# Rotary tables moved behind the last low part, x's norm spread over two engines, and idle matmuls ahead of the first products, in a two-layer decoder trunk

## The chip, the cores and the metric

The kernel runs on one core of one Trainium2 chip. Its time is the device time of one execution in microseconds (us), the median of several runs. TensorE is called PE in the profile's rows, VectorE DVE, ScalarE ACT, GpSimd POOL, SyncE SP; PEld is TensorE's loading of weights.

## The reference

Two layers of a decoder on a sequence of 512 tokens of width 2048, all in f32. The change lies in the opening of layer 0 and at the end of its first stage. Cut to what matters there:

```
c_act = silu(c)
mod = (c_act @ ada_w[i] + ada_b[i])                 # per layer: shift, scale, gate
h = rmsnorm(x, norm_g[i]) * (1.0 + scale) + shift
...
# layer 0: retention
proj = h @ w_in                                     # 2048 x (2048 q, 2048 k, 4096 v, 4096 g)
q = rope(q.reshape(B, S, RET_HEADS, RET_DK), pos)   # cos and sin of pos * inv_freq
k = rope(k.reshape(B, S, RET_HEADS, RET_DK), pos) * (RET_DK ** -0.5)
...
return (silu(g) * y) @ w_out
```

Layer 1 is a latent attention, and a last RMSNorm closes the trunk. x, the adaLN weights and a few constants also come in layouts prepared on the host (`x_t`, `ada_t`, `vecs`, `rot_c`).

## The kernel before

**Products in three parts.** Each f32 matrix is split into a high part (rounded to the fast matmul type, by a copy on ScalarE) and a low part (the rest, by a subtraction on VectorE); a product is then hi x hi, hi x lo and lo x hi. The profile shows the copies as CAST and the subtractions as TENSOR_TENSOR.

**The opening** (L439 to L556). Everything is transposed: `xT[u]` holds 2 x 128 channels of x against 512 tokens, u from 0 to 7. SP loads x, then the rows of the adaLN weights (`aw`, 1 MB each, four buffers) and the first weights (`v`, `g`, `qk`; three raw buffers). TensorE spreads c over all partitions (`c_ps`, L462), ScalarE puts it through silu into `c_all`, in four pieces. For x's norm ScalarE squares each `xT[u]` (`square`, L474), VectorE adds the squares up (`gather`), TensorE sums them over partitions into `x_sums` (`add_squares`), `rsqrt` takes the factor per token (a scaling on VectorE, a power on GpSimd), `spread_one` puts it on a diagonal (two blocks by ScalarE, two by VectorE) and TensorE spreads that over all partitions as `x_r`. `near` (tile x_near) is a copy of `x_r` in SBUF. `normalise` multiplies `xT` by it. A column of shift or scale is a weighted sum of an `aw` tile with `c_all` on VectorE (`sum_mod` whole, `sum_part` in halves), finished on ScalarE as b_col and a_col; `make_h` then makes h's high part (`hT`) and an f32 copy (`h_..f`) on ScalarE, from which VectorE makes the low part.

**The first stage** (L558 to L615) runs over eight units u of two channel blocks. Each unit multiplies h by three pieces of the input weights (the first head's q and k, its v, its g), 24 matmuls each. The 4 banks `acc` serve v and qk in turn: `swap` has ScalarE copy the partial sums out and the others back; g keeps the 4 banks `aux`. `prepare(u)` emits a unit's normalise, sums, casts and low parts, `load_unit` its loads. After unit 7, `hand_over` stores v (GpSimd's queue) and brings qk's partial sums back, and the last qk products run (`bank_products`).

**The rotary tables.** `rotary_tables` (L251) is a generator: a load of the positions, then steps of VectorE work (a multiply by the frequencies, a reduction of the angle in several parts, a clamp), at last two Sin activations on ScalarE. In the kernel before all of it is drawn in one go after `hand_over` (`for _ in tables`), the load on ScalarE's queue, and the two tables are stored to HBM by GpSimd's queue (`tables_d`).

**The order of the work.** `queued(fn)` ties each instruction that fn emits behind the last one emitted so far on its engine, for ScalarE, VectorE, TensorE and SP: each of these four queues runs in the order in which the code is written, and an instruction that waits holds up those behind it. After the first stage the memory pool `l0` is closed and `lp` opened in its place; a tile of `lp` must wait for the last user of the memory beneath it. Then a list of steps follows (the other heads' q and k, retention, layer 1); the main loop loads weights up to three units ahead and calls `prepare_for(i + 1)`, the casts and low parts of the next step, ahead of step i's matmuls. Ahead of the loop stand the first step's preparation and, by `keep_rows`, the evacuation of the first stage's banks: `qk0[b]` into tiles qk_st (0 and 2 in the pool base, 1 and 3 in `lp`), then g through silu (g_st). The first step's products take the `acc` banks as these come free.

Of the kernel before, what the change touches and what calls it, by code (L numbers as in the profile page):

```python
# [9 lines left out]
F32 = mybir.dt.float32  # L10
F32R = mybir.dt.float32r
I32 = mybir.dt.int32
# [4 lines left out]
P = 128  # L17
T = 512
# [31 lines left out]
def hybrid_trunk_kernel(  # L50
# [56 lines left out]
    def acc(name):  # L107
        return psum.tile([P, T], F32, tag="acc", bufs=4, name=name)
# [4 lines left out]
    def small(name, n=1):  # L113
        return base.tile([P, n], F32, tag="small", bufs=24, name=name)

    ident = base.tile([P, P], F32, name="ident")
# [3 lines left out]
    ones = base.tile([P, P], F32, name="ones")  # L120
    DVE.memset(ones, 1.0)
    mhalf = base.tile([P, NT], F32, name="mhalf")
# [127 lines left out]

    def rotary_tables(cos, sin, col, signed, name, queue):  # L251

        pos_i = base.tile([P, T], I32, tag="tmp", bufs=6, name=f"{name}_pi")
        queue.dma_start(pos_i, positions.rearrange("o t -> (o t)").partition_broadcast(P))
# [178 lines left out]
    def queued(fn, *args):  # L433
        with behind(A_, V_, T_, S_):
            return fn(*args)
# [24 lines left out]
    c_all = l0p.tile([P, D], F32, name="c_all")  # L460
    ACT.dma_start(c_all[0:1, :], c)
    c_ps = [acc(f"c_ps{j}") for j in range(4)]  # L462
    for j, ps in enumerate(c_ps):
# [10 lines left out]
    def square(u, j=slice(0, 2)):  # L474

        if u not in sq:
            sq[u] = k4b(f"x_sq_{u}", F32)
        ACT.activation(sq[u][:, j, :], xT[u][:, j, :], AF.Square)

# [12 lines left out]
    ret_tables = [rot(l0p, f"ret_{n}") for n in ("cos", "sin")]  # L492
    tables = rotary_tables(*ret_tables, 0, False, "ret", ACT)
    silus = {1: 0, 2: 1, 4: 2, 5: 3}
    for u in range(NU - 2):
# [6 lines left out]
    for j in range(2):  # L502
        queued(square, NU - 1, j)
    queued(gather, 0, 0, 1)
    queued(add_squares, 0, True, False)
    queued(gather, NU - 2, NU - 2, 1)
# [4 lines left out]
    def scaled_bias():  # L511
        DVE.scalar_tensor_tensor(
            out=bias1, in0=bias_c[0][:, KD:], scalar=1.0, in1=norm_c[0], op0=ALU.add, op1=ALU.mult
        )

    POOL.dma_start(c_d, c_all[0:1, :])
    queued(scaled_bias)
    queued(sum_part, 0, 0, 0)
    r_col = queued(rsqrt, x_sums[:, 0:NT], NT, 1.0 / D, "x")
    diag = tmp("x_diag")  # L520
    x_r, near = aux("x_r"), l0p.tile([P, T], F32, name="x_near")

    def spread_one(t):
        cols = slice(t * P, (t + 1) * P)
        if t % 2:
            DVE.tensor_scalar(out=diag[:, cols], in0=ident, scalar1=r_col[:, t : t + 1], scalar2=None, op0=ALU.mult)
        else:
            ACT.activation(diag[:, cols], ident, AF.Identity, scale=r_col[:, t : t + 1])
        PE.matmul(x_r[:, cols], ones, diag[:, cols], start=True, stop=True)

    def normalise(u, j=None):
# [4 lines left out]
        DVE.tensor_mul(v, v, r)  # L536

    for t in range(NT):
        queued(spread_one, t)
    low_v = queued(prepares["v", 0])  # L540
    queued(sum_part, 0, 0, 1)
    queued(sum_part, 0, 1, 0)
    queued(normalise, 0, 0)
    queued(ACT.copy, near, x_r)
    queued(sum_part, 0, 1, 1)
    low = queued(make_first, 0)
    queued(low_v)
    low_g = queued(prepares["g", 0])
    queued(low_g)
# [11 lines left out]
    def prepare(u):  # L561

        here, there = ("qk", "v") if u % 2 == 0 else ("v", "qk")
        queued(normalise, u)
# [15 lines left out]
    queued(products, "v", 0)  # L580
    queued(sum_mod, 1, 0)
    banks["g"] = [aux(f"g0_{b}") for b in range(4)]
    queued(products, "g", 0)
    queued(queued(prepares["qk", 0]))
    queued(normalise, 0, 1)
    queued(swap, "v", "qk")
    queued(sum_mod, 1, 1)
    low = queued(make_first, 1)
    queued(low)
    queued(products, "qk", 0)  # L590
    queued(products, "qk", 1)
# [4 lines left out]
    for u in range(1, NU):  # L596
# [9 lines left out]
        if more:  # L606
            queued(swap, here, there)
            prepare(u + 1)
        else:
            queued(hand_over)  # L610
            for _ in tables:
                pass
            for n, t in enumerate(ret_tables):
                POOL.dma_start(tables_d[n * P : (n + 1) * P, :], t)
        queued(bank_products, there, u)  # L615
    qk0, g0 = banks["qk"], banks["g"]
    l0.__exit__(None, None, None)


    lp = tc.tile_pool(name="lp", bufs=1)  # L620
    lpp = lp.__enter__()

# [1283 lines left out]
    n_loaded = 3  # L1906
    n_prepared = prepare_for(0)
    for b in range(4):
        queued(keep_rows, qk0[b], qk_d, b * P, f"qk0_st{b}", AF.Identity, in_turn(b))
# [276 lines left out]
```

## Time and profile before

| | |
|---|---|
| time, median of 3 runs | 2192.41 us (2191.99 to 2193.34) |
| the profiled execution: time, span | 2194.48 us, 2192.7 us |
| granted TensorE clock, mean | 0.995 |
| busy: TensorE, its weight loads, VectorE, ScalarE, GpSimd | 98%, 82%, 71%, 46%, 5% |
| HBM traffic | 200 GB/s over the span |

The span is the time from the first to the last instruction of the program; the time of an execution also holds what lies around it. A row of the timeline has the start in us, the duration in us, the engine (a q behind it: its queue issues a DMA), the line, the operation, the tiles written and read, the shapes, the number of instructions merged into the row, and in brackets how long the engine stood idle before and what it waited for. Instructions overlap by a little, so durations add up to somewhat more than the pitch of a series.

### The profile page before, as it was taken

Reading aid. Unit: us, or ns where it says so; the run is one execution under the profiler, and the core shown is the slowest. Engines: PE = TensorE matmul, PEld = TensorE weight load, DVE = VectorE, ACT = ScalarE, POOL = GpSimd, SP = SyncE. Lnnn points to the kernel's source line nnn. Section 1 sums busy time; section 2 is a strip of 40 time slices with the busy share of each in tenths; the row PEclk is TensorE's granted clock in tenths of the full one; section 3 lists DMA queues with packets and bytes.
Section 4 is the critical chain, followed back from the end, with each engine's and each line's share of the span. In section 5 each row is a group of like instructions: output and inputs, shape, how many; then the busy total and the mean of one; then the engine's idle time right before and its main releaser. Section 6 shows DMA issues by size and latency. Waiting matters only on the chain.

```text
span 2192.7 us, 27643 instructions
## 1 busy us (share of the span) xinstructions
PE 2149.2 (98%) x10176; PEld 1795.6 (82%) x10176; DVE 1563.2 (71%) x2312; ACT 1015.7 (46%) x1547; POOL 100.9 (5%) x175
## 2 busy tenths in 40 slices
PE   6998999999999999999999999999999999999997
PEld 4886888888888877888888888888888889888887
DVE  7976878677676788756677767657877677776545
ACT  6763344434343444433444535344444366664443
POOL 0001000000000000010000000010000000000000
PEclk9999999999999999999999999999999999999999
DMA  9965767767768678674646556443458723235333
GB/s 351 381 244 180 236 204 249 270 214 236 248 197 277 221 250 289 191 239 155 220 164 201 174 189 208 144 158 115 160 192 300 266 87 99 84 112 178 112 103 131
DMA packets 204970, 440.25 MB, mean 201 GB/s; under 512 B 19313, under 2 KB 56209, under 8 KB 200993
## 3 DMA queue, kind: packets, MB, share of 16 engines
q1 hardware_dynamic: 192624, 399.30, 54.9%
q0 software_dynamic: 11920, 38.91, 4.5%
q8 instruction: 79, 1.29, 0.2%
q14 instruction: 57, 0.47, 0.1%
q10 hardware_dynamic: 290, 0.27, 0.1%
HBM read 395.42 MB, written 43.00 MB: 200 GB/s over the span
## 4 chain that ended last, share of the span: by engine, by line
PE 85%; DVE 7%; issue 4%; ACT 2%; DMA 1%; POOL 0%; SPq 0%; DVEq 0%; POOLq 0%; ACTq 0%
PE o L1196 13%; PE qk L161 4%; PE qk L163 4%; PE qk L162 4%; PE o L2052 4%; PE x L744 2%; PE y L744 2%; PE y L745 2%; PE y L743 2%; PE x L745 2%; PE s L744 2%; PE s L745 2%; PE x L743 2%; PE s L743 2%; PE o L162 2%
## 5 line engine op out<-in xcount | busy, mean ns | idle before, releaser
L1196 PE MATMUL o<-o_h,o_whi 128*128 128x512 f32 (+1 forms) x496 | 192.2, 388 | 0.0
L1196 PE MATMUL o<-o_h,o_wlo 128*128 128x512 f32 (+1 forms) x496 | 191.4, 386 | 0.0
L1196 PE MATMUL o<-o_l,o_whi 128*128 128x512 f32 (+1 forms) x496 | 191.3, 386 | 0.0
L161 PE MATMUL qk<-hT,qk_h 128*128 128x512 f32 x448 | 175.9, 393 | 8.4 <-ACT qk_st L626 8.4
L162 PE MATMUL qk<-hT,qk_h 128*128 128x512 f32 x448 | 175.4, 391 | 0.0
L163 PE MATMUL qk<-hT,qk_l 128*128 128x512 f32 x448 | 175.3, 391 | 0.0
L136 DVE TENSOR_TENSOR o_wlo<-o_r,o_whi 128x1024 fp32r<-128x1024 f32 x61 | 74.6, 1224 | 80.7 <-ACT o_whi L135 80.7
L136 DVE TENSOR_TENSOR qk_l<-qk_r,qk_h 128x1024 fp32r<-128x1024 f32 x56 | 68.2, 1224 | 70.5 <-ACT qk_h L135 70.5
L1196 PEld LDWEIGHTS o<-o_h,o_wlo 128*128 128x128 f32 x496 | 93.2, 188 | 18.8
L1196 PEld LDWEIGHTS o<-o_h,o_whi 128*128 128x128 f32 x496 | 93.2, 188 | 18.3
L1196 PEld LDWEIGHTS o<-o_l,o_whi 128*128 128x128 f32 x496 | 93.2, 188 | 18.2
L161 PEld LDWEIGHTS qk<-hT,qk_h 128*128 128x128 f32 x448 | 84.8, 189 | 26.4 <-ACT qk_st L626 8.9
L163 PEld LDWEIGHTS qk<-hT,qk_l 128*128 128x128 f32 x448 | 84.6, 189 | 18.0 <-DVE qk_l L136 0.3
L162 PEld LDWEIGHTS qk<-hT,qk_h 128*128 128x128 f32 x448 | 84.8, 189 | 17.7
L161 PE MATMUL g<-h,g_h 128*128 128x512 f32 x232 | 90.6, 390 | 0.3 <-ACT g_h L135 0.3
L162 PE MATMUL g<-h,g_h 128*128 128x512 f32 x232 | 90.3, 389 | 0.0
L163 PE MATMUL g<-h,g_l 128*128 128x512 f32 x232 | 89.8, 389 | 0.0
L898 DVE SCALAR_TENSOR_TENSOR mod<-mod,c_bm 128x1024 f32<-128x1024 f32 x64 | 78.1, 1220 | 16.1 <-DMA mod<-in_ada_t_dram 16.1
L135 ACT CAST qk_h<-qk_r 128x1024 fp32r<-128x1024 f32 x56 | 57.9, 1051 | 66.4 <-PE qk L162 53.3
L135 ACT CAST o_whi<-o_r 128x1024 fp32r<-128x1024 f32 x61 | 63.6, 1053 | 20.0 <-issue 10.0
L351 DVE SCALAR_TENSOR_TENSOR aw<-aw,c_all 128x2048 f32<-128x2048 f32 x30 | 67.5, 2286 | 0.0
L136 DVE TENSOR_TENSOR o_w_lo<-o_w_raw,o_w_hi 128x1024 fp32r<-128x1024 f32 x32 | 39.0, 1221 | 37.5 <-ACT o_w_hi L135 37.5
(1259 smaller groups left out, 5986.7 us busy)
## 6 DMA issues: line engine op xcount, KB each, us to landing
mod<-in_ada_t_dram SPq DMA_DIRECT2D x128, 512.0 KB, 5.9
o_r<-in_ret_w_out_dram SPq DMA_DIRECT2D x64, 512.0 KB, 4.4
aw<-in_ada_t_dram SPq DMA_DIRECT2D x30, 1024.0 KB, 7.7
qk_r<-in_ret_w_in_dram SPq DMA_DIRECT2D x112, 256.0 KB, 3.9
g_r<-in_mla_w_in_dram SPq DMA_DIRECT2D x32, 512.0 KB, 4.4
o_w_raw<-in_mla_w_out_dram SPq DMA_DIRECT2D x32, 512.0 KB, 3.7
qk_d<-qk_st POOLq DMA_DIRECT2D x32, 256.0 KB, 3.3
qk_r<-qk_d SPq DMA_DIRECT2D x32, 256.0 KB, 6.0
```

Source lines behind the costliest of these rows:

```text
L135: ACT.copy(hi, src)
L136: DVE.tensor_sub(lo, src, hi.bitcast(F32))
L161: PE.matmul(o, lhs[0], rhs[0], start=first and not seeded, stop=False, skip_group_check=seeded)
L162: PE.matmul(o, lhs[0], rhs[1], start=False, stop=False, skip_group_check=seeded)
L163: return PE.matmul(o, lhs[1], rhs[0], start=False, stop=last, skip_group_check=seeded)
L351: DVE.scalar_tensor_tensor(out=aw, in0=aw, scalar=1.0, in1=c_all, op0=ALU.mult, op1=ALU.mult, accum_out=col,)
L743: PE.matmul(banks[b], a[0], w[0], start=first, stop=False, skip_group_check=True)
L744: PE.matmul(banks[b], a[0], w[1], start=False, stop=False, skip_group_check=True)
L745: PE.matmul(banks[b], a[1], w[0], start=False, stop=True, skip_group_check=True)
L898: DVE.scalar_tensor_tensor(out=aw, in0=aw, scalar=1.0, in1=silu_c[j], op0=ALU.mult, op1=ALU.mult, accum_out=mc[:, j, b : b + 1],)
L1196: PE.matmul(o, w[i][:, ki, c0 + b * P : c0 + (b + 1) * P], a[j], start=first and i + j == 0, stop=last and i == 1, skip_group_check=True,)
L2052: PE.matmul(banks2[b][:, cols], w[0][i][:, 0, b * P : (b + 1) * P], o2_moving(w, u, cols)[j], start=u + i + j == 0, stop=u == KD - 1 and i ...
```

## The change

1. The silu table is asked for ahead of the first square, by a silu of one column of ones (`first_silu`); the constants `ones` and `eps` are made first. The first silu of c moves up behind x's square 0.
2. The square of `xT[1]` goes from ScalarE to VectorE.
3. `x_factor` takes the place of `rsqrt` in the opening: the scaling is on ScalarE, the power stays on GpSimd. All four diagonal blocks go to ScalarE.
4. `keep_busy(n)` issues n matmuls of ones by ones (128 x 128, f32) into a bank `warm` that nobody reads: 5 ahead of the first `x_sums` products, 6 ahead of `x_r`'s, 4 behind those.
5. The order of VectorE's and ScalarE's first work changes: the half sums run ahead of the first normalise, the cast of g ahead of h's first block, the copy to `near` behind it; the normalise of unit 1 leaves `prepare(1)` and stands ahead of the low part of h's block 1.
6. The tables: the positions load goes to SP's queue and into `near`; their eight VectorE steps are emitted behind `prepare(7)`, thus behind h's last low part and ahead of unit 6's remaining products in the text; the two sines are emitted behind the first step's `prepare_for(0)`. The stores of the tables and the change of pools come after that.

```
--- before.py
+++ after.py
@@ -113,12 +113,14 @@
     def small(name, n=1):
         return base.tile([P, n], F32, tag="small", bufs=24, name=name)
 
+    ones = base.tile([P, P], F32, name="ones")
+    DVE.memset(ones, 1.0)
+    eps = base.tile([P, 1], F32, name="eps")
+    DVE.memset(eps, EPS)
     ident = base.tile([P, P], F32, name="ident")
     make_identity(nc, ident)
     mask = base.tile([P, P], F32, name="mask")
     make_causal_mask(nc, mask, mask_val=-1e30)
-    ones = base.tile([P, P], F32, name="ones")
-    DVE.memset(ones, 1.0)
     mhalf = base.tile([P, NT], F32, name="mhalf")
     DVE.memset(mhalf, -0.5)
     rt = base.tile([P, 4], F32, name="rt")
@@ -248,9 +250,9 @@
     def rot(pool, name):
         return pool.tile([P, T], F32, tag="rot", bufs=2, name=name)
 
-    def rotary_tables(cos, sin, col, signed, name, queue):
-
-        pos_i = base.tile([P, T], I32, tag="tmp", bufs=6, name=f"{name}_pi")
+    def rotary_tables(cos, sin, col, signed, name, queue, place=None):
+
+        pos_i = (place or tmp)(f"{name}_pi").bitcast(I32)
         queue.dma_start(pos_i, positions.rearrange("o t -> (o t)").partition_broadcast(P))
         r, k, kh = sin, cos, pos_i.bitcast(F32)
         yield
@@ -459,6 +461,7 @@
 
     c_all = l0p.tile([P, D], F32, name="c_all")
     ACT.dma_start(c_all[0:1, :], c)
+    ACT.activation(small("first_silu"), ones[:, 0:1], AF.Silu)
     c_ps = [acc(f"c_ps{j}") for j in range(4)]
     for j, ps in enumerate(c_ps):
         queued(PE.matmul, ps, ones[0:1, :], c_all[0:1, j * T : (j + 1) * T], True, True)
@@ -475,7 +478,10 @@
 
         if u not in sq:
             sq[u] = k4b(f"x_sq_{u}", F32)
-        ACT.activation(sq[u][:, j, :], xT[u][:, j, :], AF.Square)
+        if u == 1:
+            DVE.tensor_mul(sq[u], xT[u], xT[u])
+        else:
+            ACT.activation(sq[u][:, j, :], xT[u][:, j, :], AF.Square)
 
     def gather(to, u, j=None):
         o, i = (sq[to], sq[u]) if j is None else (sq[to][:, 0, :], sq[u][:, j, :])
@@ -490,8 +496,14 @@
 
     tables_d = dram.tile([4 * P, T], F32, name="tables_d")
     ret_tables = [rot(l0p, f"ret_{n}") for n in ("cos", "sin")]
-    tables = rotary_tables(*ret_tables, 0, False, "ret", ACT)
-    silus = {1: 0, 2: 1, 4: 2, 5: 3}
+    tables = rotary_tables(*ret_tables, 0, False, "ret", nc.sync, lambda n: near)
+    warm = aux("warm")
+
+    def keep_busy(n):
+        for _ in range(n):
+            PE.matmul(warm[:, 0:P], ones, ones, start=True, stop=True)
+
+    silus = {0: 0, 2: 1, 4: 2, 5: 3}
     for u in range(NU - 2):
         queued(square, u)
         if u in silus:
@@ -502,6 +514,7 @@
     for j in range(2):
         queued(square, NU - 1, j)
     queued(gather, 0, 0, 1)
+    queued(keep_busy, 5)
     queued(add_squares, 0, True, False)
     queued(gather, NU - 2, NU - 2, 1)
     for j in range(2):
@@ -513,19 +526,24 @@
             out=bias1, in0=bias_c[0][:, KD:], scalar=1.0, in1=norm_c[0], op0=ALU.add, op1=ALU.mult
         )
 
+    def x_factor():
+        v, r = small("x_v", NT), small("x_r", NT)
+        ACT.activation(v, x_sums[:, 0:NT], AF.Identity, bias=eps, scale=1.0 / D)
+        POOL.tensor_tensor(out=r, in0=v, in1=mhalf, op=ALU.pow)
+        return r
+
     POOL.dma_start(c_d, c_all[0:1, :])
     queued(scaled_bias)
     queued(sum_part, 0, 0, 0)
-    r_col = queued(rsqrt, x_sums[:, 0:NT], NT, 1.0 / D, "x")
+    r_col = queued(x_factor)
+    queued(keep_busy, 6)
+    queued(sum_part, 0, 0, 1)
     diag = tmp("x_diag")
     x_r, near = aux("x_r"), l0p.tile([P, T], F32, name="x_near")
 
     def spread_one(t):
         cols = slice(t * P, (t + 1) * P)
-        if t % 2:
-            DVE.tensor_scalar(out=diag[:, cols], in0=ident, scalar1=r_col[:, t : t + 1], scalar2=None, op0=ALU.mult)
-        else:
-            ACT.activation(diag[:, cols], ident, AF.Identity, scale=r_col[:, t : t + 1])
+        ACT.activation(diag[:, cols], ident, AF.Identity, scale=r_col[:, t : t + 1])
         PE.matmul(x_r[:, cols], ones, diag[:, cols], start=True, stop=True)
 
     def normalise(u, j=None):
@@ -535,17 +553,17 @@
             v, r = xT[u][:, j, :], near if j else x_r
         DVE.tensor_mul(v, v, r)
 
+    queued(sum_part, 0, 1, 0)
     for t in range(NT):
         queued(spread_one, t)
+    queued(keep_busy, 4)
     low_v = queued(prepares["v", 0])
-    queued(sum_part, 0, 0, 1)
-    queued(sum_part, 0, 1, 0)
+    queued(sum_part, 0, 1, 1)
     queued(normalise, 0, 0)
+    low_g = queued(prepares["g", 0])
+    low = queued(make_first, 0)
     queued(ACT.copy, near, x_r)
-    queued(sum_part, 0, 1, 1)
-    low = queued(make_first, 0)
     queued(low_v)
-    low_g = queued(prepares["g", 0])
     queued(low_g)
     queued(low)
 
@@ -561,7 +579,8 @@
     def prepare(u):
 
         here, there = ("qk", "v") if u % 2 == 0 else ("v", "qk")
-        queued(normalise, u)
+        if u > 1:
+            queued(normalise, u)
         for s in range(2):
             queued(sum_mod, 2 * u, s)
         queued(sum_mod, 2 * u + 1, 0)
@@ -578,16 +597,18 @@
     load_unit(1)
     swap(None, "v")
     queued(products, "v", 0)
-    queued(sum_mod, 1, 0)
     banks["g"] = [aux(f"g0_{b}") for b in range(4)]
     queued(products, "g", 0)
-    queued(queued(prepares["qk", 0]))
     queued(normalise, 0, 1)
+    queued(sum_mod, 1, 0)
+    low = queued(prepares["qk", 0])
+    queued(low)
     queued(swap, "v", "qk")
     queued(sum_mod, 1, 1)
     low = queued(make_first, 1)
+    queued(products, "qk", 0)
+    queued(normalise, 1)
     queued(low)
-    queued(products, "qk", 0)
     queued(products, "qk", 1)
     queued(products, "g", 1)
     queued(swap, "qk", "v")
@@ -608,17 +629,11 @@
             prepare(u + 1)
         else:
             queued(hand_over)
-            for _ in tables:
-                pass
-            for n, t in enumerate(ret_tables):
-                POOL.dma_start(tables_d[n * P : (n + 1) * P, :], t)
+        if u == NU - 2:
+            for _ in range(8):
+                queued(next, tables)
         queued(bank_products, there, u)
     qk0, g0 = banks["qk"], banks["g"]
-    l0.__exit__(None, None, None)
-
-
-    lp = tc.tile_pool(name="lp", bufs=1)
-    lpp = lp.__enter__()
 
     def keep_rows(ps, dst_d, r0, name, func=AF.Identity, own=None):
 
@@ -1905,6 +1920,12 @@
             load()
     n_loaded = 3
     n_prepared = prepare_for(0)
+    queued(next, tables)
+    for n, t in enumerate(ret_tables):
+        POOL.dma_start(tables_d[n * P : (n + 1) * P, :], t)
+    l0.__exit__(None, None, None)
+    lp = tc.tile_pool(name="lp", bufs=1)
+    lpp = lp.__enter__()
     for b in range(4):
         queued(keep_rows, qk0[b], qk_d, b * P, f"qk0_st{b}", AF.Identity, in_turn(b))
     for b in range(4):
```

More of the change, by code (lines that the diff above doesn't have):

```diff
@@ L492, in hybrid_trunk_kernel, with keep_busy @@
     ret_tables = [rot(l0p, f"ret_{n}") for n in ("cos", "sin")]
-    tables = rotary_tables(*ret_tables, 0, False, "ret", ACT)
-    silus = {1: 0, 2: 1, 4: 2, 5: 3}
+    tables = rotary_tables(*ret_tables, 0, False, "ret", nc.sync, lambda n: near)
+    warm = aux("warm")
+    def keep_busy(n):
+        for _ in range(n):
+            PE.matmul(warm[:, 0:P], ones, ones, start=True, stop=True)
+    silus = {0: 0, 2: 1, 4: 2, 5: 3}
     for u in range(NU - 2):
@@ L514, in scaled_bias, with x_factor @@
         )
+    def x_factor():
+        v, r = small("x_v", NT), small("x_r", NT)
+        ACT.activation(v, x_sums[:, 0:NT], AF.Identity, bias=eps, scale=1.0 / D)
+        POOL.tensor_tensor(out=r, in0=v, in1=mhalf, op=ALU.pow)
+        return r
     POOL.dma_start(c_d, c_all[0:1, :])
@@ L588, in hybrid_trunk_kernel @@
     low = queued(make_first, 1)
+    queued(products, "qk", 0)
+    queued(normalise, 1)
     queued(low)
[L590 removed]
     queued(products, "qk", 1)
@@ L610, in hybrid_trunk_kernel @@
             queued(hand_over)
[L611 to L614, printed above, removed]
+        if u == NU - 2:
+            for _ in range(8):
+                queued(next, tables)
         queued(bank_products, there, u)
     qk0, g0 = banks["qk"], banks["g"]
-    l0.__exit__(None, None, None)
-    lp = tc.tile_pool(name="lp", bufs=1)
-    lpp = lp.__enter__()
     def keep_rows(ps, dst_d, r0, name, func=AF.Identity, own=None):
@@ L1907, in hybrid_trunk_kernel @@
     n_prepared = prepare_for(0)
+    queued(next, tables)
+    for n, t in enumerate(ret_tables):
+        POOL.dma_start(tables_d[n * P : (n + 1) * P, :], t)
+    l0.__exit__(None, None, None)
+    lp = tc.tile_pool(name="lp", bufs=1)
+    lpp = lp.__enter__()
     for b in range(4):
```

44 lines of the change are left out of this document (26 added, 18 removed).

## The prediction

> **What bounds the kernel now.** I read the page, then TensorE's waits, then the timeline around the two long ones.
>
> ```profile
> span 2192.7 us, 27643 instructions
> PE 2149.2 (98%) x10176; PEld 1795.6 (82%) x10176; DVE 1563.2 (71%) x2312; ACT 1015.7 (46%) x1547; POOL 100.9 (5%) x175
> PE qk L161 <- ACT qk_st L626: 8.4, 1, 8.4
> PE x_sums L486 <- DVE x_sq L482: 4.7, 2, 4.4
> PE v L410 <- ACT hT L243: 4.6, 2, 3.7
> PE x_r L529 <- ACT x_diag L528: 1.8, 1, 1.8
> ```
>
> TensorE is busy 98% of the span, so time is only to be had where it stands idle or runs slowly. Its longest wait is one of 8.4 us, and the next lie in the opening: the change touches all four. (The waits are: what, who was waited for, total, times, longest.)
>
> **Part 1: the rotary tables.** At the hand-over from the first stage to the step list:
>
> ```profile
> 149.05 0.68 DVE L246 TENSOR_TENSOR hT<-h_15f,hT 128x512 fp32r<-128x512 f32 x1
> 160.00 0.43 DVE L257 CAST ret_sin<-ret_pi 128x512 f32<-128x512 int32 x1 [10.26 <-DMA ret_pi<-in_positions_dram]
> 169.71 0.69 DVE L277 SCALAR_TENSOR_TENSOR ret_cos<-ret_sin 128x512 f32<-128x512 f32 x1
> 156.37 0.36 ACTq L254 DMA_DIRECT2D ret_pi<-in_positions_dram  x1
> 156.67 0.62 ACT L399 COPY qk<-part_qk 128x512 f32<-128x512 f32 x1
> 170.43 0.63 ACT L279 ACTIVATE ret_sin<-ret_sin 128x512 f32<-128x512 f32 x1 [13.14 <-DVE ret_cos L277]
> 170.97 0.70 ACT L280 ACTIVATE ret_cos<-ret_cos,rt 128x512 f32<-128x512 f32 x1
> 171.58 1.03 ACT L135 CAST qk_h<-qk_r 128x1024 fp32r<-128x1024 f32 x1
> 174.57 1.57 ACT L626 ACTIVATE qk_st<-qk 128x512 f32<-128x512 f32 x3 [1.47 <-DMA tables_d<-ret_cos]
> 176.01 2.09 ACT L626 ACTIVATE g_st<-g 128x512 f32<-128x512 f32 x4
> 164.33 0.39 PE L410 MATMUL qk<-hT,qk_whi 128*128 128x512 f32 x1
> 173.15 0.80 PE L161 MATMUL qk<-hT,qk_h 128*128 128x512 f32 x1 [8.44 <-ACT qk_st L626]
> 179.13 0.39 PE L163 MATMUL qk<-hT,qk_l 128*128 128x512 f32 x1
> 173.10:178.90 5.80, 5.75 (x14) 4.42 (x15) 0.77 (x1) 4.33 (x9) 3.98 (x8) 0.50 0.88 301
> 55.75 5.61 PE L410 MATMUL g<-hT,g_k4b 128*128 128x512 f32 x24
> ```
>
> VectorE is done with h's last low part at 149.73 and idles 10.26 us, because the positions are asked for only at 156.37, behind ScalarE's copies. Its table work then takes 160.00 to 170.40, 10.4 us. ScalarE waits 13.14 us for it, makes the sines, casts, and only then evacuates the bank that TensorE wants. The window row (its length; busy time of PE, PEld, DVE, ACT, POOL; granted clock; DMA share, GB/s) shows the second price: after the pause the clock is 0.50. The fifteenth product of the step starts at 179.13, 14 x 0.427 us behind the first. At the full clock the pitch is 0.227 (last row: 24 products in 5.61 us, the last one lasting 0.39); without the pause the fifteenth would start at 164.33 + 15 x 0.227 = 167.73. The pause costs 179.13 - 167.73 = 11.4 us.
>
> After the change the positions load stands on SP behind unit 7's loads, and the 10.4 us of VectorE work directly behind the low part.
>
> ```profile
> 132.85 1.63 SPq L326 DMA_DIRECT2D qk_raw<-in_ret_w_in_dram  x2
> 144.08 5.97 SPq L685 DMA_DIRECT2D qk_r<-in_ret_w_in_dram  x6
> ```
>
> SP stands free between 134.5 and 144.08, so the load delays none of the steps' loads behind it. Its target is now x_near, last read by unit 7's normalise; the load waits for that at most, and lands some 4 us (156.37 to 160.00) later, or 8 behind the queue's backlog: before 143, against a need at 149.7. On the old clock the tables end at 149.7 + 10.4 = 160.1. ScalarE has copied until 157.3, casts the step's first weight (1.03, the sines now stand behind it), makes both sines 160.2 to 161.4 and evacuates bank 0 by 162.0. TensorE ends at 164.7 and needs the bank only then: the pause goes, and with it the cold clock. **11.4 us**.
>
> What is late next: banks 1 and 3 wait for the stores of the tables, whose memory they take (174.57 is 2.9 us behind the second sine's end, 171.67). So 161.4 + 2.9 = 164.3, three evacuations 1.57, four gates 2.09, the next cast 1.03 and its low part 1.2 give 170.2; TensorE wants that low part at 164.56 + 26 x 0.227 = 170.5. The cover is 0.3 us; should it fail, each us late costs one. I take 0 with up to 1.5 us of loss. That the first stage's memory is given up later costs nothing by itself: in both orders its last user is the tables' stores.
>
> **Part 2: the opening.**
>
> ```profile
> L435 PE MATMUL c_ps<-c_all,ones x8: 1056/1056/1187, 4.6 to 10.7; 1*128 1x512 f32 x8
> 7.16 1.28 ACT L467 ACT_TABLE_LOAD   x1
> 14.16 2.11 ACT L478 ACTIVATE x_sq<-x 128x1024 f32<-128x1024 f32 x3
> 16.77 1.49 DVE L482 TENSOR_TENSOR x_sq<-x_sq,x_sq 128x512 f32<-128x512 f32 x2
> 18.32 1.87 PE L486 MATMUL x_sums<-ones,x_sq 128*128 128x1 f32 x8 [0.33 <-DVE x_sq L482]
> 20.47 1.03 POOL L131 TENSOR_TENSOR x_r<-x_v,mhalf 128x4 f32<-128x4 f32 x1 [5.37 <-DVE x_v L129]
> 21.54 0.69 ACT L528 ACTIVATE x_diag<-ident,x_r 128x128 f32<-128x128 f32 x2 [5.27 <-POOL x_r L131]
> 21.99 2.08 PE L529 MATMUL x_r<-x_diag,ones 128*128 128x128 f32 x8 [1.80 <-ACT x_diag L528]
> 26.27 0.16 DVE L367 TENSOR_TENSOR mc_1b<-mc 128x1 f32<-128x1 f32 x1
> 26.89 0.81 ACT L243 ACTIVATE hT<-x,b_col,a_col 128x512 fp32r<-128x512 f32 x1
> 27.76 2.07 PE L410 MATMUL v<-v_whi,hT 128*128 128x512 f32 x4 [3.69 <-ACT hT L243]
> 28.31 1.03 ACT L330 CAST g_k4b<-g_raw 128x1024 fp32r<-128x1024 f32 x1
> 31.12 2.28 DVE L351 SCALAR_TENSOR_TENSOR aw<-aw,c_all 128x2048 f32<-128x2048 f32 x1
> 32.69 2.88 PE L410 MATMUL g<-hT,g_k4b 128*128 128x512 f32 x12
> 38.69 1.21 PE L410 MATMUL qk<-hT,qk_whi 128*128 128x512 f32 x4 [0.40 <-ACT hT L243]
> 39.37 0.69 DVE L246 TENSOR_TENSOR hT<-h_1f,hT 128x512 fp32r<-128x512 f32 x1 [2.01 <-ACT h_1f L245]
> 28.00:32.00 4.00, 4.00 (x10) 2.88 (x11) 2.62 (x3) 2.29 (x3) 0.00 (x0) 1.00 1.02 424
> ```
>
> From 55.75 (the row of unit 1's g products, shown above) on TensorE runs unit after unit without a wait, so the opening is worth what start that row moves to. I walked each engine's queue in program order with the durations of the rows. Walked in the old order, the last of these 24 products ends at 61.3 (row: 61.36) and the stage at 164.7 (row: 164.72), so the walk may be used for the new order:
>
> - Squares: the silu ahead of x moves the 1.28 us table load into idle time, and x's square 1 goes to VectorE (one more product like its 1.23 us sums, in time free until then). The last square ends at 15.3 instead of 16.27, no earlier, since the four silus now wait for c's products and the squares for x; VectorE's five sums and four half sums then end at 17.1 instead of 18.26, TensorE's x_sums at 19.1 instead of 20.19.
> - The mean goes to ScalarE. No row has that; I take 0.3, half the row of two diagonals, which are wider (bounds 0.1 and 0.7, and as much on v's start). The power stays 1.03 on POOL: done at 20.5 (21.50).
> - Six idle matmuls, twelve passes like x_r's at 0.213, run 18.9 to 21.45 ahead of the x_r products, whose diagonal is ready at 20.95: 0.5 us of delay, which is off the path as long as ScalarE is later (below). The five ahead of x_sums fit into TensorE's wait there (11.8 to 14.9), the four behind x_r into the wait for hT (23.2 to 24.9). x_r is complete at 23.5; normalise, which needs it, ends at 24.15.
> - VectorE no longer makes diagonals, so all four half sums end at 22.3, not 26.43, and hT waits for ScalarE alone: 20.56 + four diagonals 1.24 + two casts 1.9 + both columns 0.6 + 0.8 = 25.1. v's products start at **25.15** (27.76).
> - If the clock is up by then, the 12 products take 2.7 instead of 4.9 us: g starts at 28.1 (32.69).
> - VectorE from 24.15: two low parts 2.28, h0's 0.6, normalise 0.6, sum 2.21, qk's low 1.14, sum 2.21: 33.2. Column and hT: qk's second products start at **34.56** (38.69). The normalise moved ahead of h1's low part fills VectorE's 2.01 us wait.
> - From there the order is the old one (x_near's copy, now behind hT, ends at 26.3, before g needs x_r's bank), the weights landing in time even at 2.8 us for each load of 1 MB (the window row has 424 GB/s, 2.5 us): the 24 g products start at **51.5** (55.75). Gain **4.2 us**.
>
> The open term is the clock. The eight c products follow one another every 0.87 us from 4.6 to 10.7, none shorter than 1056 ns, so 7 us of them didn't raise it; but they use one row of the array, while the idle matmuls use 128x128 operands like the two bursts in which it rose, at 27.76 (12 products in 4.9 us, the next 12 in 2.9) and at 173.15 (5.8 us in). I take these as the nearer rows, since idle matmuls and x_r run back to back from 18.9 to 24.9. Bounds: warm already at 12, 5.5 us (the same walk, x_sums and x_r at half their time); the idle matmuls not counted, and the clock rising as late into the products as in those two bursts. At 27.76 eleven of the twelve products must have been slow, 4.5 us; at 173.15 it took 5.8. Then ten to fourteen of the 36 products ahead of qk's second ones take 0.2 us more each, and those start at 35.3 to 36.1 instead of 34.56, TensorE now the later: 3.5 to 2.7 us are left.
>
> **Sum.** 11.4 + 4.2 = 15.6 us. Against the profiled execution (2194.48 us, span 2192.7) that is 2178.9; the median of the runs, 2192.41, stands 2.1 lower: **2176.8 us**. The two parts do not overlap: everything behind 55.75 only moves forward.
>
> **Rivals.**
> 1. The idle matmuls don't count: 11.4 + 2.7 to 3.5, 2178.3 to 2177.5. For it: the c products. Against: the operands' shape.
> 2. The opening's gain is eaten by transfers or by VectorE before 55.75, whose row then stays: 11.4 alone, 2181.0. For it: the DMA share of 1.02 in the window row; against: landings with time to spare in the walk.
> 3. The tables' stores land late, so that the second step's low part misses its time: each us late costs one beyond the 0.3; at 2 us, 1.7, so 2178.5. For it: they are POOL's, issued beside VectorE's work. The Trainium skill, "SBUF — State Buffer", section "SBUF: two separate sides", lets some VectorE operations lock POOL out of writing its descriptors; no row here shows it.
> 4. The clock is up from the first c products on and never falls, as five idle matmuls fill the pause behind them: 11.4 + 5.5, 2175.5. Against: the c products' even 1056 ns. The Trainium skill, "TensorE: Matmul & The Clock Gate", section "The HAM clock gate", has it so: one busy window of about 3.4 us opens the gate, whatever the matmuls are. On that the trace disagrees, 7 us of c products at one duration.
> 5. Slower: the positions land late. VectorE waits with the step's first low part behind it, and TensorE with both. The tables may end 2.7 us later (162.0 to 164.7) before bank 0 is missed; beyond, a us costs a us, so the change is slower from 2.7 + 15.6 = 18 us on, positions landing at about 168; at 172, 2196. Against: SP's free stretch, above.
>
> **How the numbers follow.** Forecast 0.53, rival 1 0.26, rival 2 0.07, rival 3 0.07, rival 4 0.04, rival 5 0.03. The range goes from 2174.5 (rival 4, and a us for the spread of runs, 2191.99 to 2193.34) to 2181.0 (rival 2). Two thousandths, 4.4 us, is what a measurement of this kernel can tell from no change; every case but rival 5 is beyond it, with something kept for what I don't see: faster 0.95, same 0.03, slower 0.02.
>
> **What would show it.** Right: ret_sin's cast follows h_15f's low part without a wait; no wait of TensorE for qk_st; granted clock 1.00 throughout 165 to 180; one table load at the start; v's first products near 25.2 at a pitch of 0.227; unit 1's g products from about 51.5. Wrong: products at 0.427 from 25 on (rival 1), a wait for qk_l in the second step (rival 3), or VectorE's cast of the positions waiting for them (rival 5); a g row still at 55 (rival 2).

## The result, and the profile after

The changed kernel takes **2178.22 us** (median of 4 runs, 2177.25 to 2178.51), the kernel before 2192.57 (4 runs, 2191.99 to 2193.34): ratio 0.9934, interval 0.9916 to 0.9951. Run again beside two of the experiments it took 2178.48 against 2192.86, ratio 0.9934 (0.9922 to 0.9947). The profiled execution took 2178.51 us, its span is 2176.7, 16.0 less than before.

The page's first lines and TensorE's longest waits, of the kernel after (what waited, for whom, total, times, longest):

```profile
span 2176.7 us, 27707 instructions
PE 2150.4 (99%) x10206; PEld 1798.4 (83%) x10206; DVE 1563.9 (72%) x2311; ACT 1015.1 (47%) x1549; POOL 100.4 (5%) x175
PE c_ps L437 <- DMA c_all<-in_c_dram: 4.8, 1, 4.8
PE qk L163 <- ACT qk_st L641: 1.0, 1, 1.0
PE v L412 <- ACT hT L245: 0.9, 1, 0.9
```

The wait of 8.4 us for qk_st is one of 1.0; those of the opening (4.7, 4.6, 1.8) are filled with idle matmuls or, the one for hT, down to 0.9. The longest wait is now the one for c, with which the kernel starts.

The opening after, from the timeline (TensorE, then VectorE and ScalarE):

```profile
18.74 2.91 PE L504 MATMUL warm<-ones 128*128 128x128 f32 x12
21.44 1.92 PE L547 MATMUL x_r<-x_diag,ones 128*128 128x128 f32 x8
25.04 1.19 PE L412 MATMUL v<-v_whi,hT 128*128 128x512 f32 x4
28.04 2.89 PE L412 MATMUL g<-hT,g_k4b 128*128 128x512 f32 x12
34.43 1.21 PE L412 MATMUL qk<-hT,qk_whi 128*128 128x512 f32 x4 [0.79 <-ACT hT L245]
46.88 2.35 PE L412 MATMUL v<-v_whi,hT 128*128 128x512 f32 x8 [0.65 <-DVE hT L248]
50.91 1.29 PE L412 MATMUL g<-hT,g_k4b 128*128 128x512 f32 x5
23.39 0.69 DVE L554 TENSOR_TENSOR x<-x,x_r 128x512 f32<-128x512 f32 x1 [1.38 <-PE x_r L547]
18.91 0.26 ACT L531 ACTIVATE x_v<-x_sums,eps 128x4 f32<-128x4 f32 x1 [3.83 <-PE x_sums L492]
1.76 1.28 ACT L464 ACT_TABLE_LOAD   x1 [1.76 <-issue]
```

v's products start at 25.04 and four last 1.19 us, where the same four lasted 2.07 at 27.76 before: the clock is up. Unit 1's g products start at 50.91, 4.84 us earlier than before. The table load stands at 1.76, in ScalarE's idle time, and the opening has no other. The profile's column PEclk cannot be used ahead of the first recorded change of the clock: it shows 1.00 there, whatever the pitch of the matmuls. The trace also records the changes of the granted clock: the first is a rise, at 24.63 us here and at 32.15 before.

The hand-over after: VectorE, ScalarE, SP's loads, TensorE, and two windows (length; TensorE's busy time; granted clock; DMA share; GB/s):

```profile
144.20 0.69 DVE L248 TENSOR_TENSOR hT<-h_15f,hT 128x512 fp32r<-128x512 f32 x1
144.80 0.42 DVE L259 CAST ret_sin<-x_near 128x512 f32<-128x512 int32 x1
155.77 0.71 ACT L282 ACTIVATE ret_cos<-ret_cos,rt 128x512 f32<-128x512 f32 x1
156.38 0.57 ACT L641 ACTIVATE qk_st<-qk 128x512 f32<-128x512 f32 x1
161.61 1.57 ACT L641 ACTIVATE qk_st<-qk 128x512 f32<-128x512 f32 x3 [4.65 <-DMA tables_d<-ret_cos]
156.36 0.89 SPq L700 DMA_DIRECT2D qk_r<-in_ret_w_in_dram  x2
159.48 0.39 PE L412 MATMUL qk<-hT,qk_whi 128*128 128x512 f32 x1
159.71 0.39 PE L163 MATMUL qk<-hT,qk_h 128*128 128x512 f32 x1
162.26 0.50 PE L163 MATMUL qk<-hT,qk_h 128*128 128x512 f32 x1 [1.03 <-ACT qk_st L641]
164.21 0.39 PE L165 MATMUL qk<-hT,qk_l 128*128 128x512 f32 x1
165.00:170.00 5.00, 5.00 (x24) 1.00 0.97 315
170.00:180.00 10.00, 10.00 (x46) 1.00 0.42 138
```

The cast of the positions follows the low part without a wait, bank 0 is evacuated long before TensorE wants it, and TensorE goes from the stage (159.48) to the step list (159.71) without a pause, at the full clock. But banks 1 to 3 are evacuated only from 161.61 on, behind the store of ret_cos, and after six products of bank 0 TensorE waits 1.03 us for bank 1. The fifteenth product of the step list starts at 164.21 (179.13 before).

So the same product starts 4.85 us earlier at the end of the first stage and 14.92 earlier at the fifteenth product of the step list: **opening 4.85, tables 10.07**.

### The profile page after: what moved, and what is told of

It is laid out like the page before. It is cut to its first block, busy times and chain, and to the rows that moved or that the text cites. A ratio compares the mean times of both kernels' runs of the same rounds, so it can differ in the third digit from the quotient of the medians.

```text
span 2176.7 us, 27707 instructions
## 1 busy us (share of the span) xinstructions
PE 2150.4 (99%) x10206; PEld 1798.4 (83%) x10206; DVE 1563.9 (72%) x2311; ACT 1015.1 (47%) x1549; POOL 100.4 (5%) x175
## 4 chain that ended last, share of the span: by engine, by line
PE 85%; DVE 7%; issue 4%; ACT 3%; DMA 1%; POOL 0%; DVEq 0%; POOLq 0%; ACTq 0%; SPq 0%
PE o L1211 13%; PE qk L163 4%; PE qk L165 4%; PE qk L164 4%; PE o L2073 4%; PE x L759 2%; PE y L759 2%; PE y L760 2%; PE y L758 2%; PE x L760 2%; PE s L759 2%; PE s L760 2%; PE x L758 2%; PE s L758 2%; PE o L164 2%
## 5 line engine op out<-in xcount | busy, mean ns | idle before, releaser
L1211 PEld LDWEIGHTS o<-o_h,o_wlo 128*128 128x128 f32 x496 | 93.2, 188 | 18.7
```

Source lines behind the costliest of these rows:

```text
L1211: PE.matmul(o, w[i][:, ki, c0 + b * P : c0 + (b + 1) * P], a[j], start=first and i + j == 0, stop=last and i == 1, skip_group_check=True,)
```

## The experiments

**Which part brings what.** Two kernels, each with one part of the change. Only the tables (the kernel before, with this of the diff):

```
-    tables = rotary_tables(*ret_tables, 0, False, "ret", ACT)
+    tables = rotary_tables(*ret_tables, 0, False, "ret", nc.sync, lambda n: near)
...
-            for _ in tables:
-                pass
+        if u == NU - 2:
+            for _ in range(8):
+                queued(next, tables)
...
+    queued(next, tables)          # behind prepare_for(0), then the stores and the change of pools
```

> Only the rotary tables are moved; the opening is that of the kernel before. Theory (the trace of the changed kernel): the pause at the hand-over and its slow clock go, but banks 1 to 3 of qk are still evacuated late, behind the store of ret_cos, so that 10.1 of the 11.4 us are gained: 2192.4 - 10.1 = 2182.3, the fifteenth product of the step list at about 169.1, a TensorE wait of 0.8 to 1.5 us for qk_st. Rival (the prediction's sum as it stands): no such wait, 11.4 us, 2181.0, fifteenth product at 167.7. Second rival (the parts help each other: the tables gain less without the warm opening): under 8 us, 2184.4 or more.

Measured: 2184.20 us (2183.76 to 2184.54), before 2192.58 (15 runs, 2190.47 to 2194.90): ratio 0.9966 (0.9953 to 0.9978). ScalarE and TensorE at its hand-over, and a row of TensorE's waits:

```profile
167.14 1.57 ACT L620 ACTIVATE qk_st<-qk 128x512 f32<-128x512 f32 x3 [5.32 <-DMA tables_d<-ret_cos]
167.79 0.50 PE L161 MATMUL qk<-hT,qk_h 128*128 128x512 f32 x1 [1.70 <-ACT qk_st L620]
169.73 0.39 PE L163 MATMUL qk<-hT,qk_l 128*128 128x512 f32 x1
PE v L410 <- DVE hT L246: 1.3, 1, 1.3
```

The pause is gone and the wait behind the store is there, 1.70 us long; the fifteenth product stands at 169.73, a gain of 9.4. Theory upheld in kind: the wait is longer than in the changed kernel (1.70 against 1.03) and than it had said, and the median gives 8.4 us where it had 10.1 (2182.3). That time lies next to the second rival's 2184.4, but the trace shows 9.4. The prediction's 11.4 without a wait is refuted. (The last row is of the old opening, and is used below.)

Only the opening (the changed kernel, with the tables drawn and stored where the kernel before does it):

> Only the opening is changed; the rotary tables stay where the kernel before has them. Theory (the parts add up): unit 1's g products start at 50.9 and everything behind moves by the same 4.85 us, the pause of 8.4 us and its slow clock included, since the positions are asked for behind ScalarE's copies, which move too: 2192.4 - 4.85 = 2187.6, fifteenth product at 174.3. Rival (the opening's gain is lost where the pause waits for something with a time of its own, a transfer): the fifteenth product stays near 179, 2191 to 2192.4.

Measured: 2187.66 us (11 runs, 2185.74 to 2188.87), ratio 0.9979 (0.9970 to 0.9988).

```profile
21.45 1.23 PE L547 MATMUL x_r<-x_diag,ones 128*128 128x128 f32 x8
50.19 4.70 PE L412 MATMUL g<-hT,g_k4b 128*128 128x512 f32 x20
167.54 0.80 PE L163 MATMUL qk<-hT,qk_h 128*128 128x512 f32 x1 [8.39 <-ACT qk_st L647]
```

As the theory said in time (2187.6), and the pause of 8.39 us moves forward whole. The fifteenth product stands at 172.93, not at 174.3: the clock came back 4.46 us after the pause (172.00), where it took 5.77 before (178.92). Unit 1's g products start at 50.19, 0.7 us earlier than in the changed kernel, though the code up to there is the same: x_r's products already run fast here (1.23 us for eight passes, 1.92 there). The clock rose at 21.81 in this execution. The medians of the two halves give 8.4 + 4.9 = 13.3 us against 14.4 for the whole; the intervals are wide enough for the two to agree.

**The idle matmuls.** Without them, and with the same number of them at one row of operands:

```
-    queued(keep_busy, 5)          # and 6, and 4
...
-            PE.matmul(warm[:, 0:P], ones, ones, start=True, stop=True)
+            PE.matmul(warm[:, 0:P], ones[0:1, :], ones[0:1, :], start=True, stop=True)
```

> The changed kernel without its fifteen idle matmuls. Theory (they raise the clock): v's first products still start near 24.5 to 25.1, since ScalarE's columns set that, but four take about 1.9 us instead of 1.19, and the clock rises 4.5 to 5.8 us into them; unit 1's g products start 0.7 to 1.5 us later, at 51.6 to 52.4, and the time is 2178.2 + 0.7 to 1.5 = 2178.9 to 2179.7. Rival (the clock rises near 24.6 whatever runs, because TensorE has been in use since 4.8): four products in 1.2 us from the start, unit 1's g products at 50.4 to 50.9, time 2177.7 to 2178.2.

> The changed kernel with its idle matmuls at one row of operands (1x128 by 1x128, the rows of c's products) in place of 128x128; as many, and of the same length. Theory (matmuls that use one row of the array do not raise the clock; c's 7 us of them ran at one duration): as the kernel without idle matmuls, four v products in about 1.9 us, unit 1's g products at 51.6 to 52.4, 2178.9 to 2179.7. Rival (only the time in which the array is in use counts, as the Trainium skill's page TensorE: Matmul & The Clock Gate, section The HAM clock gate, has it): as the changed kernel, four v products in 1.2 us, 50.9, 2178.2.

Measured: 2178.91 us without them (2178.68 to 2179.61), 2179.63 with one row (2179.54 to 2180.64). First without them, then with one row, after that the kernel below that has only the last ten:

```profile
24.99 2.07 PE L412 MATMUL v<-v_whi,hT 128*128 128x512 f32 x4 [2.00 <-ACT hT L245]
51.60 3.11 PE L412 MATMUL g<-hT,g_k4b 128*128 128x512 f32 x13
...
23.93 2.07 PE L504 MATMUL warm<-ones 1*128 1x128 f32 x8
25.93 2.07 PE L412 MATMUL v<-v_whi,hT 128*128 128x512 f32 x4
53.19 1.52 PE L412 MATMUL g<-hT,g_k4b 128*128 128x512 f32 x6
...
25.14 1.20 PE L412 MATMUL v<-v_whi,hT 128*128 128x512 f32 x4 [0.79 <-ACT hT L245]
50.97 3.79 PE L412 MATMUL g<-hT,g_k4b 128*128 128x512 f32 x16
```

On the clock both theories hold. Without idle matmuls v's products start slow (2.07 us for four), and the clock is recorded up from 29.31, 4.3 us later; unit 1's g products move from 50.91 to 51.60. The time does not tell this from the changed kernel, whose runs reach up to 2178.97; the rows do. So of the opening's 4.84 us the idle matmuls bring 0.69 (0.4 to 1.4 over the executions with them, by where their clock rose), and the other 4.15 come from its remaining edits (points 1, 2, 3 and 5 of the change), which no run takes apart. With one row they do not raise it at all: it is recorded up from 31.63, 5.7 us into v's products, and being slow themselves they hold these back to 25.93; unit 1's g products start only at 53.19, 2.3 us later than in the changed kernel and later than the 52.4 that the theory allowed. In the median 1.2 to 1.4 of that show. One-row idle matmuls are worse here than none.

Without the first five, ahead of x_sums:

> The changed kernel without the five idle matmuls ahead of x's sums; the six ahead of x_r and the four behind it stay. Theory (TensorE in use from 18.7 to 24.9 is what raises the clock): v's four products still take 1.2 us from 25.0, unit 1's g products start at 50.9, 2178.2. Rival (the first five are needed too, the clock rises later): four v products in 1.9 us or a rise one to three us into them, g products 0.3 to 1.0 us later, 2178.5 to 2179.2.

Measured: 2178.08 us (2177.18 to 2178.86), the clock up from 23.18, g products at 50.97 (rows above). Leaving the first five out changed nothing that shows.

**When the clock rises, and what holds it.** Ten more idle matmuls ahead of c's products:

```
+    queued(keep_busy, 10)
     c_ps = [acc(f"c_ps{j}") for j in range(4)]
```

> The changed kernel with ten more idle matmuls of 128x128 ahead of c's products, where TensorE waits for c from 0.9 to 4.8 us. It asks when the clock rises and whether one-row products keep it up. Theory (128-row matmuls count, one-row matmuls do not): the clock rises between 4 and 8 us, so that some of c's eight passes last near 0.55 us instead of 1.06, and it falls again before 18, since c's products do not hold it; v's products start at 25.0 as before, and the time is 2178.2 or up to 0.5 less. Rival (once up, anything holds it): x_sums takes 1 us instead of 1.87 and x_r 1.0 instead of 1.9, unit 1's g products start near 49.6, the bound of 5.5 us that the prediction gave for a warm start, and the time is 2176.9.

Measured: 2177.46 us (2177.21 to 2178.95), not told apart from the changed kernel. Timeline, then windows (columns as above):

```profile
1.06 4.63 PE L469 MATMUL warm<-ones 128*128 128x128 f32 x20 [1.06 <-DVE mhalf L125]
5.62 3.89 PE L437 MATMUL c_ps<-c_all,ones 1*128 1x512 f32 x8
9.44 2.50 PE L469 MATMUL warm<-ones 128*128 128x128 f32 x10
6.00:9.40 3.40, 3.40 (x8) 1.00 1.03 413
9.50:12.90 3.40, 2.44 (x11) 0.50 1.02 398
```

The theory holds. The record has the clock up at 6.05, 5.0 us into the idle matmuls; c's eight passes then take 3.89 us, not 7.16. At 9.47 it falls again, though TensorE multiplied without a gap from 1.06 to 11.9: 3.413 us of c's one-row products alone were enough to lose it. The next rise, at 23.12, comes 13.653 us, four times that, after the fall. The Trainium skill, "TensorE: Matmul & The Clock Gate", section "The HAM clock gate", states a free-running window of 3413 ns; on that the trace agrees. By the same section of the Trainium skill it is time that counts, whatever is issued in it; on that this run and the one-row run disagree.

The recorded changes also show why the rise falls so differently from execution to execution. The stretches between them are whole multiples of 3.413 us (3.413, 10.24, 13.653, 136.53), and counted back from the first rise this grid lies elsewhere in each execution. In all thirteen profiles the clock rises at the end of the first interval of the grid in which products with 128 rows and 128 or more columns fill at least 2.97 of the 3.413 us. Intervals with up to 2.66 us of them did not raise it, even where one-row products or x's sums filled the rest. In the changed kernel the interval from 17.81 to 21.22 holds 2.48 us of them (from 18.74 on), the next is full, and the clock rises at 24.63; in its second profile, below, the interval begins at 18.33, holds 2.97 us, and the clock rises at 21.74. The five idle matmuls ahead of x's sums last 2.5 us, too little for an interval of their own.

**The wait behind the store.** Three ways to take it away: banks 1 and 3 evacuated into other memory, the stores on another queue, the weight loads held until the stores have landed.

```
-    ... qk_d, b * P, f"qk0_st{b}", AF.Identity, in_turn(b))
+    ... qk_d, b * P, f"qk0_st{b}", AF.Identity, tmp)
```

> The changed kernel, with banks 1 and 3 of qk evacuated into the ring of temporaries like banks 0 and 2, instead of the memory that the rotary tables leave. Theory (the wait of 1.03 us is for the store of ret_cos out of that memory): the four evacuations follow one another from 156.4 on, no wait of TensorE for qk_st, and the step list's fifteenth product starts at 159.71 + 14 x 0.227 = 162.9 instead of 164.21: 2178.2 - 1.3 = 2176.9. Rival (something else ends late next, the stores of qk_st out of the ring or the step's second low part): the wait moves to another place and the time stays within 0.5 us of 2178.2.

```
-        POOL.dma_start(tables_d[n * P : (n + 1) * P, :], t)
+        ACT.dma_start(tables_d[n * P : (n + 1) * P, :], t)
```

> The changed kernel, with the two stores of the rotary tables issued from ScalarE's queue instead of GpSimd's. Theory (the store of ret_cos lands 4.6 us after its issue because two weight loads of 256 KB are issued at the same moment): it still takes 3.5 us or more, and TensorE's wait for qk_st stays, 0.5 us or more; 2177.8 to 2178.8. Rival (GpSimd's queue is what is slow): the store lands within 2.6 us of its issue, the wait goes, 2176.9.

```
+    held = small("held")           # behind the stores, ahead of the next loads on SP
+    nc.sync.dma_start(held[0:1, :], tables_d[2 * P - 1 : 2 * P, 0:1])
```

> The changed kernel, with one small load on SP's queue, of one number out of the stored ret_cos, ahead of the two weight loads that went out beside the stores, so that these go out only when the stores have landed. Theory (contention with the weight loads): the store of ret_cos lands 2.4 to 2.8 us after its issue, near 159.3, bank 1 is evacuated near 159.9 ahead of its product at 161.1, the wait of TensorE goes, and the time is 2178.2 - 1.2 = 2177.0; the held loads are needed only by the fourth step and cost nothing. Rival (the store is slow by itself, on GpSimd's queue): it lands 4 us or more after its issue and the wait stays: 2178.2.

Measured, on one chip, where the kernel with only the last ten idle matmuls, which keeps the wait, took 2178.08: other memory **2176.03** us (2175.45 to 2177.88), stores on ScalarE's queue 2176.89 (2175.90 to 2178.58), loads held 2176.56 (2175.89 to 2177.56). The DMA issues around the hand-over (KB each, median us to landing) of the kernel before, the changed one, the one with ScalarE's queue and the one with the loads held; then ScalarE's evacuations in the last two:

```profile
tables_d<-ret_cos POOLq DMA_DIRECT2D x1, 256.0 KB, 2.4
...
qk_r<-in_ret_w_in_dram SPq DMA_DIRECT2D x2, 256.0 KB, 3.7
tables_d<-ret_cos POOLq DMA_DIRECT2D x1, 256.0 KB, 4.6
...
tables_d<-ret_cos ACTq DMA_DIRECT2D x1, 256.0 KB, 3.9
...
tables_d<-ret_cos POOLq DMA_DIRECT2D x1, 256.0 KB, 2.6
160.65 1.58 ACT L641 ACTIVATE qk_st<-qk 128x512 f32<-128x512 f32 x3 [2.98 <-DMA tables_d<-ret_cos]
159.48 1.58 ACT L641 ACTIVATE qk_st<-qk 128x512 f32<-128x512 f32 x3 [2.66 <-DMA tables_d<-ret_cos]
```

Holding two loads of 256 KB brings the store of ret_cos from 4.6 us to landing back to 2.6, on the same queue: contention with these loads is the cause, and the rival of a slow queue falls. The store of bank 0 goes out 0.53 us behind that of ret_cos in both kernels, so it is not what made the difference. From ScalarE's queue it still takes 3.9 us, as the theory said; that its wait would stay did not come true, since it landed 0.8 us earlier and the evacuation at 160.65 came just in time (0.2 us are left). With other memory the store still takes 4.7 us, and no evacuation waits for it. In all three the fifteenth product starts 3.2 to 3.4 us behind the step list's first (14 x 0.227 = 3.18), against 4.5 in the changed kernel. These 1.1 to 1.3 us are firmer than the medians, whose runs overlap with the 2177.18 to 2178.86 of the kernel that keeps the wait.

**A version from these runs**, with the changed kernel on the same chip:

```
     queued(sum_part, 0, 1, 1)
+    queued(low_v)                 # no longer behind the copy to near
     queued(normalise, 0, 0)
...  and tmp in place of in_turn(b), as above
```

> The version that the runs so far point to: the changed kernel with the four evacuations in the ring of temporaries, and in the opening the low part of v's first weights ahead of the normalise, in VectorE's idle 1.38 us before x_r is complete. Theory: the wait of TensorE for qk_st stays away (1.3 us, 2176.9 against 2178.2); VectorE's chain of 23.4 to 35.1 moves forward by 0.8 us, less 0.3 that v's first products may slip, so that qk's second products start near 33.7 instead of 34.43; 2176.0 to 2176.4. Rival (the transfers of the modulation weights, or ScalarE, set the second products): 34.4 stays, 2176.9.

> The changed kernel as it is, on the chip of the two runs beside it, so that their times can be set against its own: 2178.2, unit 1's g products between 50.2 and 51.2 as the clock's rise falls, a wait of TensorE for qk_st of 0.8 to 1.7 us, fifteenth product 4.5 us behind the step list's first.

Measured: 2176.40 us (2175.68 to 2176.83) against the changed kernel's 2178.48 (2176.29 to 2178.97); ratios to before 0.9926 (0.9912 to 0.9939) and 0.9934. The evacuation holds its 1.3 us; the opening's part misses. First VectorE and TensorE of the new version, then the changed kernel again:

```profile
22.71 1.22 DVE L334 TENSOR_TENSOR v_wlo<-v_raw,v_whi 128x1024 fp32r<-128x1024 f32 x1 [0.57 <-ACT v_whi L332]
23.85 0.68 DVE L554 TENSOR_TENSOR x<-x,x_r 128x512 f32<-128x512 f32 x1
26.18 0.69 DVE L248 TENSOR_TENSOR hT<-h_0f,hT 128x512 fp32r<-128x512 f32 x1 [0.51 <-ACT h_0f L247]
34.36 1.20 PE L412 MATMUL qk<-hT,qk_whi 128*128 128x512 f32 x4 [0.37 <-ACT hT L245]
...
21.47 1.19 PE L547 MATMUL x_r<-x_diag,ones 128*128 128x128 f32 x8
33.76 1.20 PE L412 MATMUL qk<-hT,qk_whi 128*128 128x512 f32 x4 [0.37 <-ACT hT L245]
50.23 4.47 PE L412 MATMUL g<-hT,g_k4b 128*128 128x512 f32 x19
```

VectorE's idle 1.38 us was filled, but v's low part itself waited 0.57 us for ScalarE's cast and pushed the normalise from 23.39 to 23.85. So h's first block came later and VectorE then waited 0.51 us for it: qk's second products stand at 34.36, 0.1 less. The changed kernel, on its own second profile, is at 33.76 without any edit, because its clock rose at 21.74. The reordering brought nothing that shows, so other memory alone is enough. Of the 2.1 us that the two versions with other memory stand, each on its own chip, below a kernel with the wait (2176.03 and 2178.08, 2176.40 and 2178.48) the traces show 1.3 to 1.4.

## Why the prediction was right, point by point

The time fell within its range, 1.4 us above its 2176.8, and faster was right. That the sum came so near is in part luck: it had 1.3 us too much for the tables and 0.6 too little for the opening. The time alone would fit rival 1 (2177.5 to 2178.3) and rival 3 (2178.5) better than the forecast; the traces tell them apart. Of the signs given for being right, "no wait of TensorE for qk_st" did not come true (1.03 us).

1. **Tables, order of the work: right.** VectorE's cast follows the low part at once (144.80), no pause, clock 1.00 from 165 to 180. The positions landed 6.6 us after their issue at 129.91, ahead of the need.
2. **Tables, the next thing late: mis-sized.** The term was 11.4 and measured 10.07. The step that failed is "161.4 + 2.9", the evacuations that follow the tables' stores, timed as in the kernel before. There the next two weight loads followed 1.9 us behind the store's issue (173.89 against 171.97). Here VectorE's low part frees a raw weight buffer at 156.33, the two loads go out at 156.36, 0.4 us ahead of the store (156.77), and the store of ret_cos took 4.6 us instead of 2.4: the evacuations start 5.1 us behind the second sine's end (161.61 - 156.48). And the first to miss them was not the second step's low part, with 0.3 us of cover, but bank 1, which TensorE wants 6 x 0.227 = 1.36 us after bank 0. The working sized what the moved load does to SP's other loads, not what those do to the moved stores. The 1.5 us of loss that it allowed for hold the 1.3.
3. **Rival 3: its event came, its place and cause did not.** The Trainium skill, "SBUF — State Buffer", section "SBUF: two separate sides", was part of its reason: VectorE locking GpSimd out of its descriptors. VectorE stood idle from 156.33 to 166.10, all through the late store, and the held loads cured it.
4. **Opening: right, low by 0.6.** Predicted 51.5 for unit 1's g products, measured 50.91 and 50.23; v's first at 25.04 (25.15), g at 28.04 (28.1), qk's second at 34.43 (34.56). The mean on ScalarE took 0.26 (taken as 0.3), the normalise starts at 23.39 (23.5). Up to there the walk is right to 0.13 us in this execution. Behind it, it kept TensorE's old wait for VectorE ahead of unit 1's products; with unit 1's normalise (1.22 us) moved ahead on VectorE, that wait is 0.65 us where the only-tables kernel, with the old opening, still has 1.3. Where the clock rises early (21.74) x_r is done 0.7 us sooner, and so are qk's second products (33.76) and unit 1's g products (50.23), though v's first start only 0.15 us sooner (24.89). So the 0.13 us hold for one place of the clock's grid, and that it fell there was luck.
5. **The clock: right**, and for the reason given, the operands' shape; rival 1 is refuted by the rise at 24.63, ahead of v's products, against 29.31 without idle matmuls, and the one-row run shows that the shape decides. Rival 4 is refuted by c's passes, which last 7.16 us in the changed kernel too, and by the fall of the clock under them.
6. **Median against profile: the last 1.4 us.** Against the profiled execution the sum gave 2178.9, and 2178.51 was measured. But of these 16.0 us only 14.92 stand at the step list's fifteenth product, where the sum had 15.6; the other 1.0 came behind it. The 2.1 us by which the profiled execution of before stood above its median were taken off again; that of after stands 0.3 above its own. From that product to the start of TensorE's last, where the code is the same but for addresses, it is 2004.3 us before, 2003.3 after, and 2001.5 to 2004.3 over all profiles of this study. What differs visibly is TensorE's wait for VectorE's low parts of the other heads' v and g (`vg_..l`): 2.0 us before, 1.6 after, 0.3 in the second profile of the changed kernel. What makes it differ stays open.

## What to carry to other kernels

A transfer that is moved takes the landing time of its new neighbours: list what else is issued in its 3 us, on every queue, before a landing from the old place is used, and look which user of its memory comes first. Idle matmuls of 128 rows raised the clock and those of one row did not (heights between were not tried), and a lead of some 6 us ahead of the first product covered the rise in all nine executions that had it. An evacuation that waits for a store can be given memory that no store still reads; here that was worth as much as holding the loads back, and the store could stay slow.

## What the runs showed of the hardware

- One-row matmuls (1x128 by 1x512, 1x128 by 1x128) neither raised nor held the granted clock: up at 6.05 us behind 128-row idle matmuls, down at 9.47 with TensorE never idle.
- The granted clock changed on a grid of 3.413 us (3.413 and 13.653 in one run, 10.24 before). In nine executions with the idle matmuls ahead of x_r, begun at 18.7 to 19.2, it rose 3.0 to 6.1 us later (21.74 to 25.08), at the end of the first interval with at least 2.97 us of 128-row products; v's products, at 24.9 to 25.5, came 0.2 to 3.2 us behind it, and unit 1's g products spread from 50.2 to 51.2.
- x's sums, matmuls of one column, did not count towards the rise: 3.7 us of them, behind 2.5 us of idle matmuls, did not raise the clock, nor did the interval from 17.81 to 21.22, which they and 2.48 us of idle matmuls fill.
- Two loads of 256 KB, issued within 0.5 us of a store of 256 KB, took it from 2.6 to 4.6 us to landing.
